# A decoder layer on one core: the SBUF layout of its matmul operands is changed

## The chip, the core and the metric

The kernel runs on one core of a Trainium2 chip. The metric is the time of one execution on the device in microseconds; lower is better. Of the core's engines, TensorE (PE) multiplies, VectorE (DVE) and ScalarE (ACT) work elementwise, GpSimd (POOL) does a few elementwise steps, and SyncE (SP) issues nearly all transfers from HBM into SBUF. PE reads its two operands from SBUF, the stationary one (a weight load, shown as PEld) and the moving one, and adds into PSUM.

## The reference, cut to what matters

One layer for 256 tokens of width 2048, all in float32 (S = 256, D = 2048, F = 5632):

```
h      = rms(x, norm1_g)
u, v, q, k, vr, g = split(h @ w_in)                # w_in: 2048 x 6144
y      = concat(spatial_gate(u, v), retention(q, k, vr, g))
x      = x + y @ w_out                             # 2048 x 2048
h2     = rms(x, norm2_g)
a      = silu(h2 @ w_gate) * (h2 @ w_up)           # two of 2048 x 5632
x      = x + a @ w_down                            # 5632 x 2048
return rms(x, final_norm_g)
```

The spatial gate and the retention work on chunks of 128 tokens and 8 heads each with 128 x 128 products; all else is the four large products.

## The kernel before

**One product as three.** A float32 product is made of three matmuls in the type float32r. Both factors are split: `hi` is the value cast to float32r, `lo` the rest. PE then adds `hi*hi`, `hi*lo` and `lo*hi` into one PSUM bank, always through the helper `mm` (line 42). The activations are the stationary factor (128 x 128, 512 bytes in each partition), the weights the moving one (128 x 512, 2048 bytes in each partition). `split` (line 44) makes `hi` on ScalarE (line 50) and `lo` on VectorE (line 51), into tiles of 1024 columns from a pool with four buffers each; the raw weights come in 1 MB tiles `raw` with three buffers (line 56).

**The stages.** `gemm_tok` (line 98) makes 12 blocks of 512 columns of w_in, with the activations in the tiles hT0 to hT3 (both parts of each), and then 4 blocks of w_out, with the activations in mT0 to mT3. Between them the small float32 products and transposes of the mixer are set in, on tiles `work` of 512 columns. `quad` (line 499) makes the FFN: 11 rounds over w_gate and w_up together, hT now holding h2, and 2 over w_down, with the split activations in hT0 to hT2.

**Seven for eight.** In each of the 11 rounds three of the eight pairs of row blocks (SEVEN_GU) go through `pair_seven` (line 471): sums and differences of the blocks are made first and seven products are taken for eight, as in Strassen's scheme. Four of the seven (3, 5, 7 and 6) have sums of activations as their stationary factor; these lie, split, in three tiles h2s1, h2s3 and h2s5 made once. Products 3, 5 and 7 follow each other, nine matmuls in a row. The tiles mT0 to mT3 serve as scratch there.

**What sets the order.** The engines work through their lists in the order in which the code is written; waits between them follow from the tiles. Where a tile lies in SBUF is set by the pools: a pool's tiles follow each other from its start, in the order of their first use, and the pools follow each other in the order in which they are opened. In the kernel before, the pool `base` is the first (line 36): the large tiles x, hT and mT (lines 87 to 89), then small ones (head, ident, ones, sums of squares, the scratch of the root), then `wp` (line 37) with raw, hi and lo, then the pool of the stage, `mix` (line 136) or `ff` (line 458).

Of the kernel before, what the change touches and what calls it, by code (L numbers as in the profile page):

```python
# [8 lines left out]
F32 = mybir.dt.float32  # L9
F32R = mybir.dt.float32r  # L10
# [5 lines left out]
P = 128  # L16
S = 256
NT = S // P
D = 2048
# [5 lines left out]
NC = 512  # L25
HC = NC // P
NF = DFF // NC
EPS = 1e-6
SEVEN_GU = (1, 3, 5)
WARM = 10  # L30

# [1 line left out]
@with_exitstack  # L33
def block_kernel(ctx: ExitStack, tc: tile.TileContext, a: dict, out: bass.AP):
    nc = tc.nc
    base = ctx.enter_context(tc.tile_pool(name="base", bufs=1))
    wp = ctx.enter_context(tc.tile_pool(name="wp", bufs=3))
    acc = ctx.enter_context(tc.tile_pool(name="acc", bufs=4, space=PSUM))
    sm = ctx.enter_context(tc.tile_pool(name="sm", bufs=4, space=PSUM))

# [19 lines left out]
    def rsqrt(v, n, pool):  # L60

        t = pool.tile([P, n], I32, name="rs_t", bufs=2, padded_shape=[P, 8])
        y = pool.tile([P, n], I32, name="rs_y", bufs=2, padded_shape=[P, 8])
        w = pool.tile([P, n], F32, name="rs_w", bufs=2, padded_shape=[P, 8])
        nc.vector.tensor_single_scalar(t, v.bitcast(I32), 1, op=ALU.logical_shift_right)
        nc.vector.tensor_scalar(out=y, in0=t, scalar1=-1.0, scalar2=float(0x5F3759DF), op0=ALU.mult, op1=ALU.add)
        yf = y.bitcast(F32)
        for i in range(3):
            r = pool.tile([P, n], F32, name="rs_r", bufs=6, padded_shape=[P, 8])
            nc.vector.tensor_tensor(out=w, in0=yf, in1=yf, op=ALU.mult)  # L70
            nc.vector.scalar_tensor_tensor(out=w, in0=w, scalar=-0.5, in1=v, op0=ALU.mult, op1=ALU.mult)  # L71
            nc.vector.scalar_tensor_tensor(out=r, in0=w, scalar=1.5, in1=yf, op0=ALU.add, op1=ALU.mult)  # L72
            yf = r
        return yf

    def row_rstd(parts, pool):
# [3 lines left out]
        nc.vector.tensor_reduce(out=v, in_=parts[:, 0:n - 1], op=ALU.add, axis=mybir.AxisListType.X)  # L80
        nc.vector.tensor_scalar(out=v, in0=v, scalar1=1.0 / D, scalar2=EPS, op0=ALU.mult, op1=ALU.add)
        w = pool.tile([P, 1], F32, name="rs_u", bufs=2)
# [1 line left out]
            out=w, in0=parts[:, n - 1:n], scalar1=1.0 / D, scalar2=v, op0=ALU.mult, op1=ALU.add)  # L84
        return rsqrt(w, 1, pool)

    x_sb = [base.tile([P, D], F32, name=f"x{n}") for n in range(NT)]
    hT = [base.tile([P, 4, 2 * S], F32R, name=f"hT{i}") for i in range(4)]
    mT = [base.tile([P, 4, 2 * S], F32R, name=f"mT{i}") for i in range(4)]
    head = base.tile([P, 2 * KD + 2 * S], F32, name="head")  # L90
    cols = head[:, 0:2 * KD]
    ident = base.tile([P, P], F32, name="ident")
# [144 lines left out]
    def norm_heads(src, dst, gi, half):  # L237
# [6 lines left out]
        for h in range(HC):  # L244
            nc.vector.bn_aggr(out=mv[:, h, :], in_=st[:, h, :])
        nc.vector.tensor_scalar(out=v, in0=mv[:, :, 1], scalar1=EPS, scalar2=None, op0=ALU.add)  # L246
        r = rsqrt(v, HC, mix)
# [180 lines left out]
    def turn_x(c):  # L428
        for half in range(2):
# [14 lines left out]
            p = 2 * c + half  # L444
            if p in SEVEN_GU:
                hf = ff.tile([P, 2, S], F32, name="hf", bufs=1)
# [5 lines left out]
    for c in range(4):  # L452
# [3 lines left out]
        if c == 0:  # L456
            p1.close()
            ff = ctx.enter_context(tc.tile_pool(name="ff", bufs=1))
            h2s = {p: ff.tile([P, 2, 4, P], F32R, name=f"h2s{p}") for p in SEVEN_GU}

# [4 lines left out]
    def pair_classic(src):  # L465

        return load_piece(src)

    odd = itertools.count()

    def pair_seven(src):

        raw = wp.tile([P, 2048], F32, name="raw", bufs=3)
        nc.sync.dma_start(raw, src)
        b12, b22, b21 = raw[:, 0:NC], raw[:, 2 * NC:3 * NC], raw[:, 3 * NC:]
        t = base.tile([P, 4 * NC], F32, name=f"mT{next(odd) % 2}")
        t13, t24 = t[:, 0:2 * NC], t[:, 2 * NC:]
        (plain,) = split(raw[:, NC:3 * NC], 2 * NC, 2 * NC)
        nc.vector.tensor_tensor(  # L479
            out=t13.rearrange("p (b c) -> p b c", b=2), in0=b12.unsqueeze(1).broadcast_to([P, 2, NC]),  # L480
            in1=raw[:, NC:3 * NC].rearrange("p (b c) -> p b c", b=2), op=ALU.subtract)
        nc.vector.tensor_tensor(out=t24[:, 0:NC], in0=b22, in1=t13[:, 0:NC], op=ALU.subtract)
        nc.vector.tensor_tensor(out=t24[:, NC:], in0=b21, in1=t24[:, 0:NC], op=ALU.subtract)
        (one,) = split(t13, 2 * NC, 2 * NC)
        (last,) = split(b21, NC, NC)
        (two,) = split(t24, 2 * NC, 2 * NC)
        cut = lambda part, h: tuple(x[:, h * NC:(h + 1) * NC] for x in part)
        return {1: cut(plain, 0), 3: cut(plain, 1), 5: cut(one, 0), 7: cut(one, 1),
                6: cut(two, 0), 4: cut(two, 1), 2: cut(last, 0)}
# [7 lines left out]
    odd_quad = itertools.count()  # L497

    def quad(src, order, seven, left, forms, todo=(), apart=0):


        todo = dict(todo)
        bank = {k: acc.tile([P, NC], F32, name="acc") for k in ("11", "12", "21", "22")}
        begun, mixed = set(), {}
        last7 = max([i for i, p in enumerate(order) if p in seven], default=-1)
        classic_left = [p for p in order if p not in seven]
        if seven:
            for k in (1, 5, 7, 6):
                bank[k] = sm.tile([P, NC], F32, name="sm")
        where = {1: 1, 2: "11", 3: "12", 4: "21", 5: 5, 6: 6, 7: 7}  # L510

        def go(b, l, r, stop):
            three(bank[b], l, r, b not in begun, stop)
            begun.add(b)

        kept = []
        for i, p in enumerate(order):
            for f in todo.get(i, ()):
                f()
            if p in seven:  # L520
                right = pair_seven(src(p))
                for k in (1, 3, 5, 7, 2, 6, 4) if i else (1, 5, 7, 6, 3, 2, 4):
                    whole = i == len(order) - 1 if isinstance(where[k], str) else i == last7
                    go(where[k], forms(p, k), right[k], whole)
                if i == last7:
                    t = base.tile([P, 4, NC], F32, name=f"mT{2 + next(odd_quad) % 2}")
                    t1, v, w, z = (t[:, i, :] for i in range(4))
                    nc.scalar.copy(t1, bank[1])
                    nc.vector.tensor_tensor(out=v, in0=bank[6], in1=t1, op=ALU.add)
                    nc.vector.tensor_tensor(out=w, in0=bank[5], in1=v, op=ALU.add)  # L530
                    nc.vector.tensor_tensor(out=z, in0=bank[7], in1=w, op=ALU.add)
                    nc.vector.tensor_tensor(out=v, in0=bank[7], in1=v, op=ALU.add)
                    mixed = {"11": t1, "12": w, "21": v, "22": z}
                continue
            (h0, l0), (h1, l1) = pair_classic(src(p))
            cut = lambda h, l, c: (h[:, c * NC:(c + 1) * NC], l[:, c * NC:(c + 1) * NC])
            right = {"12": cut(h0, l0, 0), "11": cut(h0, l0, 1), "22": cut(h1, l1, 0), "21": cut(h1, l1, 1)}
            todo_rows = [(p, right, i == len(order) - 1)]
            if i >= len(order) - apart:
                kept += todo_rows  # L540
                if i < len(order) - 1:
                    continue
                todo_rows, kept = kept, []
            for r in "12":
                for p_, right_, end in todo_rows:
                    for m in "12":
                        for c in "12":
                            go(r + c, left(p_, r + m), right_[m + c], end and m == "2")
        return bank, mixed
# [53 lines left out]
    for j in range(NF):  # L603
# [3 lines left out]
        else:  # L607
            todo[6] = [waiting]
        bank, mixed = quad(lambda p: a["w_gu"][j, p], range(KD // 2), SEVEN_GU, h2_left, h2_forms, todo)
        rows = finish_up(j, bank, mixed)  # L610
        waiting = lambda j=j, rows=rows: turn_a(j, rows)

    gf = base.tile([P, D], F32, name="hT3")
    nc.gpsimd.dma_start(gf, a["gf"].partition_broadcast(P))  # L614

    def a_split():

        made = {}

        def at(k, r):  # L620
            j = k // 4
            if j not in made:
                h = base.tile([P, 2, 4, S], F32R, name=f"hT{next(odd) % 3}")
                hi, lo = h[:, 0], h[:, 1]
                nc.scalar.copy(hi, af[j])  # L625
                nc.vector.tensor_tensor(out=lo, in0=af[j], in1=hi.bitcast(F32), op=ALU.subtract)  # L626
                made[j] = hi, lo
            return tuple(x[:, k % 4, r * P:(r + 1) * P] for x in made[j])

        return left_of(at)  # L630
# [116 lines left out]
```

## Time and profile before

| | |
|---|---|
| median of 3 runs | 1134.43 us (1134.06 to 1135.79) |
| the profiled execution | 1135.27 us, with a span of 1133.0 us |
| mean granted clock of TensorE | 0.995 of full speed |
| PE busy | 1116.5 us, 4937 instructions |
| VectorE busy | 814.0 us |
| ScalarE busy | 570.4 us |
| moved | 217.64 MB, 192 GB/s over the span |

The span runs from the first to the last instruction. Busy time is what an engine's own instructions cover; the chain that ended last is followed back from the last instruction, at each step to what released it, so its shares say on what the end rests. A PE instruction's duration covers the way through the array and overlaps the next one, so the pace of matmuls is read from how many start in a stretch, not from the mean of one.

### The profile page before, as it was taken

The page shows a single profiled execution, that of the slowest core. Times are in us where ns is not written, and L with a number is a line of the kernel's source. Part 1 is how long each engine was busy: PE and PEld are TensorE (multiplying, and loading weights), DVE is VectorE, ACT ScalarE, POOL GpSimd, SP SyncE. Part 2 cuts the span into 40 slices and gives each one's busy share as a digit, 9 for nine tenths or more (in the row PEclk, how much of TensorE's full clock was granted, in tenths as well). Part 3 has the DMA queues.
Part 4 walks back from the last instruction along what each step waited for, and adds up shares of the span by engine and source line. Part 5 has one row for each costly group of instructions (what it writes and reads, how often), then busy time and mean ns, then how long its engine had stood idle before and what let it go on. Part 6 is the DMA issues. An engine that isn't in the chain of part 4 may idle for free.

```text
span 1133.0 us, 12891 instructions
## 1 busy us (share of the span) xinstructions
PE 1116.5 (99%) x4937; PEld 901.4 (80%) x4937; DVE 814.0 (72%) x1097; ACT 570.4 (50%) x664; POOL 53.9 (5%) x36
## 2 busy tenths in 40 slices
PE   9989999999999999999999999999999999999996
PEld 7868888888888888888888888888888888888884
DVE  6896458476556689889888888888798555565555
ACT  6633434444345555556555555655656454454443
POOL 0051014011000000000000000000000000020000
PEclk9999999999999999999999999999999999999998
DMA  9845544445555445555645545555556555555551
GB/s 357 318 168 207 184 170 165 169 149 188 183 186 186 173 167 194 209 185 187 222 169 192 206 176 189 212 192 187 189 188 227 214 186 186 186 188 187 187 181 74
DMA packets 32749, 217.64 MB, mean 192 GB/s; under 512 B 3760, under 2 KB 4144, under 8 KB 7088
## 3 DMA queue, kind: packets, MB, share of 16 engines
q1 hardware_dynamic: 32544, 215.78, 53.5%
q0 software_dynamic: 144, 1.05, 0.2%
q8 instruction: 38, 0.62, 0.2%
q14 instruction: 23, 0.19, 0.0%
HBM read 214.72 MB, written 2.10 MB: 191 GB/s over the span
## 4 chain that ended last, share of the span: by engine, by line
PE 95%; DVE 3%; DMA 1%; ACT 1%; SPq 0%; issue 0%; DVEq 0%; ACTq 0%
PE acc L42 84%; PE sm L42 9%; PE sm L593 1%; DMA raw<-in_w_in 1%; DVE lo L51 1%; PE sm L434 0%; PE sm L329 0%; DVE rs_r L72 0%; DVE rs_w L71 0%; DVE work L249 0%; ACT junk L213 0%; PE sm L375 0%; ACT hi L50 0%; DVE var L246 0%; DVE x L648 0%
## 5 line engine op out<-in xcount | busy, mean ns | idle before, releaser
L42 PE MATMUL acc<-hi,hT 128*128 128x512 f32 x2484 | 799.6, 396 | 1.5 <-ACT hi L50 1.5
L51 DVE TENSOR_TENSOR lo<-raw,hi 128x1024 fp32r<-128x1024 f32 (+1 forms) x396 | 466.3, 1190 | 271.0 <-ACT hi L50 268.5
L50 ACT CAST hi<-raw 128x1024 fp32r<-128x1024 f32 (+1 forms) x396 | 395.8, 1009 | 466.1 <-PE acc L42 442.0
L42 PEld LDWEIGHTS acc<-hi,hT 128*128 128x128 f32 x2484 | 467.0, 188 | 113.5 <-ACT hi L50 2.2
L42 PE MATMUL acc<-lo,hT 128*128 128x512 f32 x1242 | 493.5, 397 | 3.4 <-DVE lo L51 3.4
L42 PEld LDWEIGHTS acc<-lo,hT 128*128 128x128 f32 x1242 | 233.6, 188 | 60.7 <-DVE lo L51 5.3
L51 DVE TENSOR_TENSOR lo<-mT,hi 128x1024 fp32r<-128x1024 f32 x66 | 80.7, 1223 | 18.2 <-ACT hi L50 18.0
L50 ACT CAST hi<-mT 128x1024 fp32r<-128x1024 f32 x66 | 69.4, 1051 | 33.2 <-PE acc L42 31.7
L42 PE MATMUL acc<-hi,mT 128*128 128x512 f32 x256 | 81.6, 396 | 0.1
L42 PE MATMUL sm<-hi,h2s 128*128 128x512 f32 x198 | 72.8, 394 | 0.0
L42 PEld LDWEIGHTS acc<-hi,mT 128*128 128x128 f32 x256 | 48.1, 188 | 12.0 <-ACT mT L378 0.5
L42 PE MATMUL acc<-lo,mT 128*128 128x512 f32 x128 | 50.5, 396 | 0.0
L42 PEld LDWEIGHTS sm<-hi,h2s 128*128 128x128 f32 x198 | 37.1, 188 | 9.0
L479 DVE TENSOR_TENSOR mT<-raw 128x1024 f32<-128x1024 f32 x33 | 40.3, 1222 | 1.0 <-DMA raw<-in_w_gu 0.5
L42 PE MATMUL sm<-lo,h2s 128*128 128x512 f32 x99 | 39.2, 396 | 0.0
L614 POOL DMA_DIRECT2D hT<-in_gf x1 | 0.7, 720 | 614.6 <-DVE mT L577 614.6
L42 PEld LDWEIGHTS acc<-lo,mT 128*128 128x128 f32 x128 | 24.0, 188 | 5.6
L626 DVE TENSOR_TENSOR hT<-af,hT 128x1024 fp32r<-128x1024 f32 x22 | 27.9, 1269 | 0.7 <-ACT hT L625 0.7
L582 ACT ACTIVATE sg<-mT,rstd 128x512 f32<-128x512 f32 x22 | 15.9, 723 | 24.0 <-DVE mT L577 24.0
L42 PE MATMUL acc<-hi,h2s 128*128 128x512 f32 x66 | 25.9, 392 | 0.0
L42 PE MATMUL sm<-hi,hT 128*128 128x512 f32 x66 | 25.9, 392 | 0.0
L625 ACT CAST hT<-af 128x1024 fp32r<-128x1024 f32 x22 | 22.9, 1042 | 0.0
(99 smaller groups left out, 545.1 us busy)
## 6 DMA issues: line engine op xcount, KB each, us to landing
raw<-in_w_gu SPq DMA_DIRECT2D x88, 1024.0 KB, 4.7
raw<-in_w_in SPq DMA_DIRECT2D x47, 1024.0 KB, 4.8
raw<-in_w_down SPq DMA_DIRECT2D x44, 1024.0 KB, 4.7
raw<-in_w_out SPq DMA_DIRECT2D x16, 1024.0 KB, 4.8
x<-in_x SPq DMA_DIRECT2D x2, 1024.0 KB, 9.2
gains<-in_gains SPq DMA_DIRECT2D x2, 1024.0 KB, 6.9
out<-x SPq DMA_DIRECT2D x8, 256.0 KB, 2.6
work<-in_xT SPq DMA_DIRECT2D x7, 256.0 KB, 7.7
```

The source lines that it names most:

```text
L42: nc.tensor.matmul(o, lhsT=l, rhs=r, start=start, stop=stop)
L50: nc.scalar.copy(hi, src[:, c:c + step])
L51: nc.vector.tensor_tensor(out=lo, in0=src[:, c:c + step], in1=hi.bitcast(F32), op=ALU.subtract)
L479: nc.vector.tensor_tensor(out=t13.rearrange("p (b c) -> p b c", b=2), in0=b12.unsqueeze(1).broadcast_to([P, 2, NC]), in1=raw[:, NC:3 * NC] ...
L582: nc.scalar.activation(sg, g, AF.Silu, scale=rstd2[r])
L593: nc.tensor.transpose(ps[:, q * S + n * P:q * S + (n + 1) * P], rows[n][:, f * P:(f + 1) * P], ident)
L614: nc.gpsimd.dma_start(gf, a["gf"].partition_broadcast(P))
L625: nc.scalar.copy(hi, af[j])
L626: nc.vector.tensor_tensor(out=lo, in0=af[j], in1=hi.bitcast(F32), op=ALU.subtract)
```

## The change

The constants `PAD_BIG` and `PAD_BASE` are new. A new pool `big` is opened first and takes x, hT and mT, behind a pad of 480 float32 columns; then comes `wp`, unchanged; then `base` with the small tiles, behind a pad of 40 columns; then the pool of the stage. Places that use the tiles of hT and mT again name the new pool. Tiles, sizes, number of buffers, engines and instructions are the same: on each of the five engines the list of instructions stands in the same order with the same waits; only the running numbers of the tiles are five higher.

```
+PAD_BIG = 480
+PAD_BASE = 40
...
+    big = ctx.enter_context(tc.tile_pool(name="big", bufs=1))
+    wp = ctx.enter_context(tc.tile_pool(name="wp", bufs=3))
     base = ctx.enter_context(tc.tile_pool(name="base", bufs=1))
-    wp = ctx.enter_context(tc.tile_pool(name="wp", bufs=3))
...
-    x_sb = [base.tile([P, D], F32, name=f"x{n}") for n in range(NT)]
-    hT = [base.tile([P, 4, 2 * S], F32R, name=f"hT{i}") for i in range(4)]
-    mT = [base.tile([P, 4, 2 * S], F32R, name=f"mT{i}") for i in range(4)]
+    big.tile([P, PAD_BIG], F32, name="pad_big")
+    base.tile([P, PAD_BASE], F32, name="pad_base")
+    x_sb = [big.tile([P, D], F32, name=f"x{n}") for n in range(NT)]
+    hT = [big.tile([P, 4, 2 * S], F32R, name=f"hT{i}") for i in range(4)]
+    mT = [big.tile([P, 4, 2 * S], F32R, name=f"mT{i}") for i in range(4)]
...
-        t = base.tile([P, 4 * NC], F32, name=f"mT{next(odd) % 2}")
+        t = big.tile([P, 4 * NC], F32, name=f"mT{next(odd) % 2}")
...
-    gf = base.tile([P, D], F32, name="hT3")
+    gf = big.tile([P, D], F32, name="hT3")
```

Where the tiles start in each partition, in bytes, in the two built programs:

| tile | used as | before | modulo 2048 | modulo 512 | after | modulo 2048 | modulo 512 |
|---|---|---|---|---|---|---|---|
| hT0 | stationary, float32r | 32896 | 128 | 128 | 34816 | 0 | 0 |
| mT0 | stationary, float32r | 65664 | 128 | 128 | 67584 | 0 | 0 |
| raw, first | weights as loaded | 102368 | 2016 | 480 | 100352 | 0 | 0 |
| hi, first | moving, float32r | 126944 | 2016 | 480 | 124928 | 0 | 0 |
| lo, first | moving, float32r | 143328 | 2016 | 480 | 141312 | 0 | 0 |
| h2s1 | stationary, float32r | 160736 | 992 | 480 | 162816 | 1024 | 0 |
| af0 | FFN activations, float32 | 177120 | 992 | 480 | 179200 | 1024 | 0 |
| ident | moving, float32 | 100608 | 256 | 256 | 161056 | 1312 | 288 |
| work, first | both, float32 | 160768 | 1024 | 0 | 162848 | 1056 | 32 |

The further tiles of a kind follow in steps of 8192 (hT, mT, raw), 4096 (hi, lo, h2s, af) and 2048 bytes (work).

## Rows read from the trace of the kernel before

**Rows 1.** The chain that ended last: shares of the span by engine, by line.
```profile
PE 95%; DVE 3%; DMA 1%; ACT 1%; SPq 0%; issue 0%; DVEq 0%; ACTq 0%
PE acc L42 84%; PE sm L42 9%; PE sm L593 1%; DMA raw<-in_w_in 1%; DVE lo L51 1%; PE sm L434 0%; PE sm L329 0%; DVE rs_r L72 0%; DVE rs_w L71 0%; DVE work L249 0%; ACT junk L213 0%; PE sm L375 0%; ACT hi L50 0%; DVE var L246 0%; DVE x L648 0%
```

**Rows 2.** Pieces of that chain, long ones: start us, us, what.
```profile
4.50 8.18 DMA raw<-in_w_in
...
119.81 22.40 PE acc L42 x96
...
361.88 22.41 PE acc L42 x96
...
909.78 206.53 PE acc L42 x885
```

**Rows 3.** Busy time by stretch: its length, each engine, clock, DMA share, GB/s.
```profile
25.00:50.00 25.00, 25.00 (x109) 20.10 (x108) 18.72 (x71) 16.12 (x27) 0.00 (x0) 1.00 0.85 334
...
700.00:800.00 100.00, 100.00 (x440) 80.51 (x439) 87.09 (x97) 57.17 (x63) 0.00 (x0) 1.00 0.53 188
1000.00:1100.00 100.00, 100.00 (x430) 80.47 (x429) 56.52 (x47) 47.19 (x49) 3.43 (x3) 1.00 0.52 186
```

**Rows 4.** Pieces of the chain around products 3, 5 and 7 (h2s).
```profile
403.36 1.37 PE sm L42 x6
...
446.20 0.69 PE acc L42 x3
446.89 1.39 PE sm L42 x6
448.29 0.70 PE acc L42 x3
...
449.69 6.30 PE acc L42 x27
```

**Rows 5.** Pieces of the chain: small float32 products, transposes.
```profile
93.86 0.87 PE sm L329 x8
...
142.21 2.68 PE sm L42 x24
```

**Rows 6.** A matmul and the next weight load in order of time: start, us.
```profile
200.04 0.62 PE L42 MATMUL acc<-hi,hT 128*128 128x512 f32 x2
200.04 0.19 PEld L42 LDWEIGHTS acc<-hi,hT 128*128 128x128 f32 x1
```

**Rows 7.** PE's instructions by form: count, busy us, mean ns of one.
```profile
L42 PEld LDWEIGHTS acc<-hi,hT 128*128 128x128 f32 x2484 | 467.0, 188 | 113.5 <-ACT hi L50 2.2
...
L42 PE MATMUL sm<-hi,h2s 128*128 128x512 f32 x198 | 72.8, 394 | 0.0
...
L42 PE MATMUL sm<-lo,h2s 128*128 128x512 f32 x99 | 39.2, 396 | 0.0
...
L42 PE MATMUL acc<-hi,h2s 128*128 128x512 f32 x66 | 25.9, 392 | 0.0
...
L42 PE MATMUL acc<-lo,h2s 128*128 128x512 f32 x33 | 13.1, 397 | 0.0
...
L42 PEld LDWEIGHTS sm<-work 128*128 128x128 f32 x96 | 11.3, 192 | 0.4
```

**Rows 8.** VectorE's instructions by form, 1024 columns: count, busy us, mean ns.
```profile
L51 DVE TENSOR_TENSOR lo<-raw,hi 128x1024 fp32r<-128x1024 f32 x355 | 438.2, 1247 | 228.9 <-ACT hi L50 227.5
...
L51 DVE TENSOR_TENSOR lo<-mT,hi 128x1024 fp32r<-128x1024 f32 x66 | 80.7, 1223 | 18.2 <-ACT hi L50 18.0
...
L626 DVE TENSOR_TENSOR hT<-af,hT 128x1024 fp32r<-128x1024 f32 x22 | 27.9, 1269 | 0.7 <-ACT hT L625 0.7
```

**Rows 9.** Who waited for whom: us in total, times, longest.
```profile
ACT hi L50 <- PE acc L42: 473.7, 319, 5.5
...
PE acc L42 <- DVE lo L51: 3.4, 3, 1.9
```

**Rows 10.** Transfers by line: count, KB each, median us from issue to landing.
```profile
raw<-in_w_down SPq DMA_DIRECT2D x44, 1024.0 KB, 4.7
...
hT<-in_gf POOLq DMA_DIRECT2D x1, 1024.0 KB, 5.2
```

More of the change, by code (lines that the diff above doesn't have):

```diff
@@ L525, in quad @@
                 if i == last7:
-                    t = base.tile([P, 4, NC], F32, name=f"mT{2 + next(odd_quad) % 2}")
+                    t = big.tile([P, 4, NC], F32, name=f"mT{2 + next(odd_quad) % 2}")
                     t1, v, w, z = (t[:, i, :] for i in range(4))
@@ L622, in at @@
             if j not in made:
-                h = base.tile([P, 2, 4, S], F32R, name=f"hT{next(odd) % 3}")
+                h = big.tile([P, 2, 4, S], F32R, name=f"hT{next(odd) % 3}")
                 hi, lo = h[:, 0], h[:, 1]
```

## The prediction

> **What bounds the kernel now.** I read the chain of work that ended last first, then its pieces in order of time, then busy time by stretch, then single forms of instructions. "Phase" below is a tile's start address modulo 512 bytes, from the address table in the section on the change.
>
> TensorE is 95% of the chain, and the helper line 42 alone, on the two kinds of PSUM tile, is 84% + 9% [rows 1]. 93% of the 1133.0 us span is 1054 us; with the granted clock at 1.00 in the stretches of [rows 3], the engine is at its 2.4 GHz level there and does not stand. So the time is the pace of the matmuls, and little else. The reader is to see in [rows 2] that the pace is one number: 96 matmuls in 22.40 us is 233.3 ns each, with tile hT stationary; 22.41 us with mT stationary; 885 in 206.53 us is 233.4 ns near the end. 512 columns at 2.4 GHz would be 213.3 ns, so each matmul carries 20 ns that are not columns.
>
> What else runs beside does not touch this pace: the DMA share goes from 0.85 to 0.52 and VectorE's busy time from 87 to 57 us per 100, while PE is busy in all of each stretch [rows 3]. The other engines follow PE: ScalarE's high parts wait 473.7 us for PE to free a buffer, PE's matmuls wait 3.4 us for VectorE's low parts [rows 9]. A change of layout can therefore move the time in one way that counts: by the 20 ns.
>
> **The change part by part.**
>
> *Instructions.* None is added, removed or moved; every engine's list is the same but for tile numbers, and every wait with it. The removal of a wait, or a new one, costs 0 because there is none.
>
> *Stationary and moving operands of the float32r matmuls.* Before, the moving operand (hi, lo) always starts at phase 480; the stationary one starts at phase 128 in hT and mT and at phase 480 in the three sum tiles h2s. After, all start at phase 0. So before has two kinds of matmul: phases that differ (hT, mT) and phases that coincide (h2s), and after has only the second kind, though at another place. [Rows 4] show what that is worth in one Strassen-like piece: the matmuls of h2s come as 3 in 0.69 us and 6 in 1.39 us, 2.08 us for 9 or 231.1 ns; by the starts (446.20 to 448.29) 2.09 us or 232.2 ns. The 27 that follow, with hT stationary, take 6.30 us, 233.3 ns. In another piece the 6 take 1.37 us, 228.3 ns. I take 231.5 ns for coinciding phases, 1.8 ns under 233.3 (0.8%).
>
> How many would gain: of 1054 us on line 42 I take off 128 small float32 matmuls (24 take 2.68 us, 111.7 ns each [rows 5], so 14.3 us) and the 198 + 99 + 66 + 33 = 396 matmuls with h2s [rows 7], which have that pace already (396 x 231.5 ns = 91.7 us). That leaves 948 us, and 0.8% of it is 7.3 us (948 x 1.8 / 233.3). That is the term of the forecast: -7.3 us. Its ends: 0 if the h2s tiles are quicker for another reason (their phase 480 itself, or that they lie some 100 KB higher than hT), and then these 396 could lose their 1.8 ns, +0.7 us; and on the other side the whole of the 20 ns, 948 x 20 / 233.3 = -81 us, because no row shows a moving operand of 512 columns at any other phase than 480. Above, the nearest row is the 4 ns that a weight load takes longer where everything starts at phase 0 (192 against 188 ns [rows 7]): 948 + 92 us, times 4 / 233.3, is +17.8 us. I take the value that a row of the same kind of matmul shows.
>
> *The small float32 matmuls and transposes.* The work tiles go the other way, from phase 0 to phase 32, ident from 256 to 288. At phase 0 moving, 111.7 ns; transposes with ident moving at phase 256, 8 in 0.87 us or 108.8 ns [rows 5]. The 2.9 ns between is the bound on both sides: 128 x 2.9 ns = 0.4 us more or less; I take 0.
>
> *VectorE and ScalarE.* Their operands change phase too. Forms of 1024 columns whose operands' phases agree (raw, hi, lo, all 480) take 1247 ns, mixed ones (mT 128, hi 480) 1223 ns, and hT 128 with af 480 take 1269 ns [rows 8]: a spread of 46 ns with no order in it by phase. At worst 355 low parts by 22 ns and 66 by 46 ns, 10.8 us over the whole span, 1% on VectorE's 87 us per 100 in its fullest stretch [rows 3]. PE's matmuls cover it: VectorE would have to become 14% slower to be the bound. 0 on the path.
>
> *DMA.* Weight rows land at 32 modulo 64 before and at a multiple of 2048 after. Only the first pieces are on the chain, 8.18 us [rows 2]; later ones land while PE works. No row has the same transfer at two addresses. The nearest are transfers of 1024 KB that land at phase 480 (raw, 4.7 us) and at phase 128 (the gains in hT3, 5.2 us, issued from another queue) [rows 10]: a tenth, so 0.8 us of the 8.18 either way at most, and I take 0.
>
> A page bears on this one. The Trainium skill, "DMA: Bandwidth & Descriptors", section "How a descriptor splits into AXI transactions", says that a descriptor not starting on a multiple of 256 bytes pays an extra transaction for the start. By it a 2048-byte row at 224 modulo 256 takes 9 transactions for 8; my estimate from that page is up to a tenth of 8.18 us, 0.8 us, so the sum would be 0.8 us lower. No row of this trace shows it.
>
> *Sum.* The profiled execution took 1135.27 us, its span 1133.0, and the median of the three runs is 1134.43. The term is made on the span and taken from the median: 1134.4 - 7.3 = 1127.1, and I forecast 1127 us.
>
> **The rivals.**
>
> *No change: 1134.* For it: the pace with hT is the same whether the stationary slice starts at 128, 640, 1152 or 1664 modulo 2048, and the same for hT and mT, 32 KB apart [rows 2]; so most address changes that the trace contains do nothing. Against it: h2s is not at 233.3. If its gain is from its own phase, the sum is +0.7 and at most 0.4 from the small ones, 1134 to 1135.5.
>
> The Trainium skill speaks for this rival: "SBUF — State Buffer", section "Specifications (TRN2)", gives lines of 16 bytes, where each cross to a new line pays a penalty. All starts were multiples of 32 before and are after, so by that rule no operand crosses more lines than it did, and the time would be 1134. The trace agrees for hT and mT, whose paces are equal [rows 2], and disagrees by 0.8% for h2s [rows 4].
>
> *The moving operand's start is most of the 20 ns: 1066.* A float32 matmul of 128 columns that starts at phase 0 has 111.7 ns, 5.0 more than 106.7 (twice 128 columns at 2.4 GHz). If float32r then also carried 5 ns and not 20, the gain is 948 + 92 us times 15 / 233.3, 67 us, so 1067. A third of it gives 1112. Against it: transposes whose moving operand starts at phase 256, off every multiple of 512, are no slower, so a start that is off a multiple costs nothing there.
>
> "TensorE: Matmul & The Clock Gate", section "Back-to-back issue gap", in the Trainium skill gives about 216 ns for 512 columns when issued back to back. By it, 17 of the 20 ns are an extra of this kernel, and the time would be 1040 x 17.3 / 233.3 = 77 us lower, an estimate from that page. The trace does not reach it anywhere: its quickest pieces are at 228 ns.
>
> *Slower: 1152.* The load of the next weights starts with the matmul (200.04 us both, [rows 6]) and takes 188 ns of the 233. Now both read streams begin at the same offset of 2048 bytes, always. If they meet in the same part of the memory and take turns, the load is longer, as in the phase-0 rows (192 ns against 188 [rows 7]), and a load that ends 4 ns later may hold the next matmul by as much: +17.8 us, 1152. It decides from the point where the load has no slack; it has 45 ns now, which speaks against, and so do the h2s matmuls, which coincide modulo 512 and are the quickest. Halfway, 1143.
>
> That the change does not do what it says is excluded: the addresses in the table are those of the built program.
>
> **How the numbers follow.** Chances: the forecast (all matmuls at the pace of h2s, 1122 to 1131) 0.35; no change 0.34; the large gain (under 1122) 0.14; slower 0.17. Forecast and no change are nearly equal; the gains together are likelier than either, so the time is that of the likelier gain. About 0.2% (2.3 us) is what a measurement of this kernel can tell from no change. Faster by more: 0.35 + 0.14 less what of the forecast's case ends within 2.3 us (0.03), 0.46. Within: 0.34 + 0.03, 0.37. Slower: 0.17. The range for 8 in 10 leaves out the deep part of the large gain (below 1108, about 0.1) and the far half of the slower case (above 1141, about 0.09). The forecast's own range is 1122 to 1131.
>
> **What would show it.** Right: in the pieces of the chain 96 matmuls with hT take 22.2 us and the last long piece loses 1.6 us of 206.5, while the h2s pieces stay at 1.39 us and the forms of VectorE within the spread of [rows 8]. No change: 22.40 us again, and h2s pieces at 1.40. Large gain: 22.40 us falls to 21 or below, and then VectorE's waits for PE shrink in the middle stretches, where it has least room. Slower: 22.4 grows and weight loads show more than 188 ns. I am wrong in mechanism, whatever the time, if the pace of hT stays and the time moves, for then a stretch without line 42 did it.

## The result and the profile after

The changed kernel takes 1107.77 us (median of 4 runs, 1106.7 to 1108.37) against 1134.98 us for the kernel before in the same runs (median of 4): 0.9759 of it, with a 95% interval of 0.9743 to 0.9776, or 27.2 us less. The forecast was 1127 us. The profiled execution took 1108.35 us, with a span of 1106.1 us. One profiled execution in the experiments below, that of the third, took 3223 us, and no figure here is made from it. Lines of the program stand 3 to 5 further down: line 42 is now 45, lines 50 and 51 are 53 and 54.

The chain by engine still is TensorE [rows 1]:

```profile
PE 95%; DVE 2%; DMA 1%; ACT 0%; SPq 0%; issue 0%; DVEq 0%; ACTq 0%
```

Its long pieces in order of time (start us, us, what) answer to [rows 2], and the one of 24 small matmuls to [rows 5]:

```profile
4.49 8.43 DMA raw<-in_w_in
...
73.40 12.62 PE acc L45 x47
...
118.59 21.80 PE acc L45 x96
140.39 2.68 PE sm L45 x24
...
354.51 21.80 PE acc L45 x96
...
888.87 200.66 PE acc L45 x885
```

96 matmuls take 21.80 us where they took 22.40, and 885 take 200.66 where they took 206.53: 226.7 ns each, 6.6 less than 233.3. The small float32 matmuls keep their 2.68 us for 24 (two instructions for each of 12 in the code), although their tiles moved from a multiple of 512 to 32 past it. Around products 3, 5 and 7 (to [rows 4]):

```profile
436.77 0.68 PE acc L45 x3
437.45 1.36 PE sm L45 x6
438.81 0.68 PE acc L45 x3
...
440.17 6.12 PE acc L45 x27
```

The h2s matmuls, which I expected to stay at 1.39 us for 6, went to 1.36: they have the same 226.7 ns as all others now. Product 6 has sums as its stationary factor too, but only three matmuls, and they stand alone between matmuls of hT. [Rows 4] leave it out; here it is, before and after:

```profile
448.99 0.70 PE sm L42 x3
...
439.49 0.68 PE sm L45 x3
```

Before, these three were as slow as hT, 0.70 us or 233 ns each, although their starts agreed. Weight loads by form [rows 7] and VectorE's forms [rows 8] (count, busy us, mean ns of one):

```profile
L45 PEld LDWEIGHTS acc<-hi,hT 128*128 128x128 f32 x2484 | 467.3, 188 | 98.4 <-ACT hi L53 2.3
...
L54 DVE TENSOR_TENSOR lo<-raw,hi 128x1024 fp32r<-128x1024 f32 x355 | 435.2, 1239 | 213.9 <-ACT hi L53 207.5
...
L54 DVE TENSOR_TENSOR lo<-mT,hi 128x1024 fp32r<-128x1024 f32 x66 | 80.6, 1220 | 16.1 <-ACT hi L53 16.1
...
L631 DVE TENSOR_TENSOR hT<-af,hT 128x1024 fp32r<-128x1024 f32 x22 | 27.9, 1267 | 0.7 <-ACT hT L630 0.7
```

A weight load still takes 188 ns, and VectorE's forms are within 8 ns of what they were. What moved the time is the pace of the float32r matmuls. Priced with the prediction's own shares, 948 us x 6.6 / 233.3 and 92 us of h2s x 4.8 / 231.5 are 26.8 + 1.9 = 28.7 us; the span lost 26.9. Most of the rest stays in the first 120 us: the piece that starts there starts 1.2 us earlier (118.59 for 119.81), where the pace alone would give up to 3.0 us on the 106 us since the first matmul of the chain. Before 73 us PE waits for VectorE's chain of statistics, so the next long piece begins at 73.40 us instead of 73.69; before it read:

```profile
73.69 12.78 PE acc L42 x47
```

### The profile page after: what moved, and what is told of

The parts are those of the page before. It is cut to its first block, busy times and chain, and to the rows that moved or that the text cites. A ratio compares the mean times of both kernels' runs of the same rounds, so it can differ in the third digit from the quotient of the medians.

```text
span 1106.1 us, 12891 instructions
## 1 busy us (share of the span) xinstructions
PE 1088.6 (98%) x4937; PEld 901.6 (82%) x4937; DVE 810.6 (73%) x1097; ACT 570.2 (52%) x664; POOL 55.0 (5%) x36
## 4 chain that ended last, share of the span: by engine, by line
PE 95%; DVE 2%; DMA 1%; ACT 0%; SPq 0%; issue 0%; DVEq 0%; ACTq 0%
PE acc L45 84%; PE sm L45 9%; PE sm L598 1%; DMA raw<-in_w_in 1%; DVE lo L54 1%; PE sm L439 0%; PE sm L334 0%; ACT junk L218 0%; DVE rs_r L75 0%; DVE rs_w L74 0%; PE sm L380 0%; DVE work L254 0%; DVE x L653 0%; SPq L168 0%; DVE rs_w L73 0%
## 5 line engine op out<-in xcount | busy, mean ns | idle before, releaser
L45 PE MATMUL acc<-hi,hT 128*128 128x512 f32 x2484 | 786.6, 391 | 1.9 <-ACT hi L53 1.9
L45 PE MATMUL acc<-lo,hT 128*128 128x512 f32 x1242 | 484.7, 390 | 4.1 <-DVE lo L54 4.1
L258 POOL TENSOR_TENSOR work<-work,gains 128x512 f32<-128x512 f32 x8 | 17.5, 2192 | 124.1 <-DVE work L254 62.1
```

Of the source, the lines that this page charges most:

```text
L45: nc.tensor.matmul(o, lhsT=l, rhs=r, start=start, stop=stop)
L258: nc.gpsimd.tensor_tensor(out=dst, in0=dst, in1=gains[gi][:, 0, cs], op=ALU.mult)
```

## The experiments

For the theories, d is the start of the stationary operand less that of the moving one, modulo 256 bytes. Before, d is 160 for hT and mT (128 - 224) and 0 for h2s (224 - 224). After, it is 0 everywhere. The first four runs were made to tell whether the moving operand alone, the stationary one alone or the pair decides.

**Moving operands 32 bytes off.**

```
-PAD_BASE = 40
+PAD_BASE = 32
+    wp.tile([P, 8], F32, name="pad_wp", bufs=1)        # opens the pool of weight buffers
```

> The changed layout with 32 bytes put ahead of the weight buffers: hi, lo and raw start at 32 modulo 2048, everything else stays where the change put it (stationary tiles at multiples of 512). Theory M (the start of the moving operand modulo 64 decides; one that is off by 32 costs 16 columns): 96 matmuls take 22.4 us again (233.3 ns each), time 1132 to 1137 us. Rival C (what counts is that the two operands start at the same offset modulo 512): now they differ everywhere, also slow, 1132 to 1137 us, and the sum products are slow as well, at 1.40 us for 6. Rival S (the stationary tiles alone made the gain): 21.8 us for 96, 1106 to 1110 us.

Measured: 1135.4 us, 0.9996 of before (0.9987 to 1.0005). The long last piece of the chain and one of h2s:

```profile
446.81 1.40 PE sm L45 x6
...
910.11 206.51 PE acc L45 x885
```

All of the gain is gone, at 233.3 ns, h2s included. Theories M and C both expected this; theory S, the stationary tiles alone, is out.

**Stationary tiles at eight starts, moving ones at 0.** hT and mT are made one by one with a pad ahead of each:

```
...
+    for name, cols in (("hT0", 0), ("hT1", 8), ("hT2", 24), ("hT3", 56), ("mT0", 8), ("mT1", 8), ("mT2", 8), ("mT3", 48)):
+        if cols:
+            big.tile([P, cols], F32, name=f"pad_{name}")
+        (hT if name[0] == "h" else mT).append(big.tile([P, 4, 2 * S], F32R, name=name))
...
```

> The changed layout, moving operands kept on multiples of 2048, but the stationary tiles each at its own start modulo 512: hT0 to hT3 at 128, 160, 256 and 480, mT0 to mT3 at 0, 32, 64 and 256. Theory M: every one of the eight at 226.7 ns, 24 matmuls of each in 5.44 us, time 1106 to 1110 us. Rival C: only mT0 at 226.7 ns, the others near 233; time about 1130. Rival S: those at 0, 64, 128 and 256 at 226.7, those at 32, 160 and 480 (off a multiple of 64) at 233 ns; about 1120 us.

Measured: 1126.95 us, 0.9931 (0.991 to 0.9952), a time that none of the three theories gave. From the chain, 24 matmuls each of hT3 (start 480), hT0 (128) and mT3 (256), in this order:

```profile
123.62 5.60 PE acc L44 x24
...
129.22 5.59 PE acc L44 x24
...
305.78 5.47 PE acc L44 x24
```

5.47 us is 228 ns, the others 233. So the moving operand's start is not enough either: theory M is out. Rival S is out too, since 128 is slow. The moving operands stay where they are in this kernel and the pace goes with the stationary tile, so it is not the writing or the landing of the weights that sets it. 256 is nearly as good as 0 (228 ns for mT3, 226.7 for mT0, which follows it), so rival C is left, with 256 in place of 512.

The h2s tiles lie at 0 here, so they match; what differs is the hT tile before and behind them. Six matmuls of products 5 and 7 between those of hT0 (128), of hT1 (160) and of hT2 (256):

```profile
443.02 1.37 PE sm L44 x6
...
453.48 1.39 PE sm L44 x6
...
463.81 1.36 PE sm L44 x6
```

With the same matching starts, nine h2s matmuls run at 232 ns between neighbours that are off by 160, at about 227.5 between neighbours off by 128, and at 226.7 between neighbours that match; this holds for all rounds but the first.

**Moving operands 64 bytes off.** As the first, with 16 columns and 24.

> The changed layout with 64 bytes put ahead of the weight buffers: hi, lo and raw start at 64 modulo 2048. Theory M in its form with 64 bytes: 226.7 ns, 1106 to 1110 us, although every moving operand now runs over a multiple of 2048, 512 and 256. Theory M with a larger unit (128 bytes or more): 233.3 ns, 1132 to 1137 us. Rival C: the operands' offsets differ by 64, so near 233 ns, 1132 to 1137 us.

Measured: 1115.36 us (the median of three executions, 1115.24 to 1118.8), 0.9834 (0.9813 to 0.9855), between the two values that the theories allowed. The 1117 us that an expectation below names for this kernel is the median with the 3223 us counted in. There is no trace of one of the three. 20.1 us less than before, over the 4605 float32r matmuls, is 4.4 ns each, so 229 ns a matmul if all have it; the mix below shows which pairs have that.

**The old order with 32 bytes.**

```
+    wp.tile([P, 8], F32, name="pad_wp", bufs=1)        # in the kernel before
```

> The kernel before with one edit: a pad of 8 float32 columns (32 bytes) ahead of the weight buffers, which brings hi, lo and raw from 2016 to 0 modulo 2048; hT and mT stay at 128 modulo 512, the order of the pools is the old one, small tiles shift by 32 bytes. Theory M: the whole gain, 1106 to 1110 us. Rival C: hT and mT still differ from the moving ones, so no gain there, 1132 to 1137 us. Rival O (the order of the pools, large tiles first, matters): 1132 to 1137 us.

Measured: 1131.09 us, 0.9966 (0.9952 to 0.9979). The end piece:

```profile
906.48 205.67 PE acc L42 x885
```

232.4 ns, 1.0 less than before: with d = 128 the moving operands on multiples of 2048 bring little, and the whole gain of theory M is not there. The h2s tiles came to 0 by the same pad, so they match, and 6 of theirs take 1.37 us, 228 ns each, between neighbours that do not match:

```profile
445.54 1.37 PE sm L42 x6
```

Both are part of the 4 us gained, which put the time a little under the 1132 us of the rivals. That left theory K, equal starts modulo 256 wherever they lie, against theory A, each operand on a multiple of its own.

**The moving operands at 128, 32, 64 and 256, with eight starts of stationary tiles.** One kernel each; the diff is that of the second experiment with other pads.

> The changed layout with the eight stationary tiles at eight starts modulo 512: hT0 to hT3 at 128, 256, 0 and 64, mT0 to mT3 at 160, 384, 480 and 32, and hi, lo and raw at 128 modulo 2048; the sum tiles h2s at 0. Read are the paces of each tile's matmuls. Theory K (the two operands must start at the same offset modulo 256, wherever that is): hT0 (128) and mT1 (384) at 226.7 ns, all others near 233, h2s too. Theory A (each operand for itself must start on a multiple of its own unit, 256 bytes for the stationary one, 64 or 256 for the moving one): hT0 and mT1 near 233 ns; with a moving unit of 64 or 128 hT1, hT2 and h2s (256, 0, 0) at 226.7, with 256 nothing at 226.7.

> As the kernel with the moving operands at 128, but hi, lo and raw at 32 modulo 2048. Theory K: only mT3 (32) at 226.7 ns. Theory A: nothing at 226.7 ns, all near 233, mT3 included.

> As the kernel with the moving operands at 128, but hi, lo and raw at 64 modulo 2048. Theory K: only hT3 (64) at 226.7 ns. Theory A with a moving unit of 64: hT1, hT2 and h2s at 226.7 ns and hT3 near 233; with a larger unit hT1, hT2 and h2s between 227 and 233, as the first kernel with 64 (time 1117 us) lets expect, and hT3 slower than these.

> As the kernel with the moving operands at 128, but hi, lo and raw at 256 modulo 2048. Theory K and theory A with a unit of 256 or less: hT1, hT2 and h2s (256, 0, 0) at 226.7 ns, all others near 233. If the moving operand needs a multiple of 512 or 2048, nothing is at 226.7 ns.

Measured: 1126.2, 1135.47, 1125.72 and 1120.7 us (0.9924, 1.0003, 0.9924 and 0.988 of before, each with an interval of at most 0.003 to either side). Pieces of the chain with 24 matmuls of one tile. Moving at 128, stationary at 64, 128 and 256:

```profile
175.10 5.50 PE acc L44 x24
...
180.59 5.46 PE acc L44 x24
...
186.06 5.58 PE acc L44 x24
```

Moving at 32, stationary at 128 and 32:

```profile
132.28 5.61 PE acc L44 x24
...
309.71 5.44 PE acc L44 x24
```

Moving at 256, stationary (hT1) at 256:

```profile
135.67 5.45 PE acc L44 x24
```

The pair 32 and 32, off every multiple of 64, is as quick as the pair 256 and 256, and 128 with 256, both on multiples of 128, is slow. So theory A is out and theory K is met, with one exception: it expected 233 ns for all pairs that differ, and 64 with 128 (d = 192) took 5.50 us, 229 ns. By d, the pace of every 24 matmuls in a row of one tile with no gap over 260 ns between two starts, after 120 us, in these four kernels and in the second (time from the first start to the last in the trace, over 23; ns):

| d | 0 | 32 | 64 | 96 | 128 | 160 | 192 | 224 |
|---|---|---|---|---|---|---|---|---|
| median | 226.9 | 233.2 | 233.4 | 234.0 | 232.7 | 233.4 | 229.3 | 233.3 |
| lowest | 226.7 | 233.1 | 232.9 | 232.2 | 232.1 | 233.0 | 228.7 | 232.8 |
| highest | 228.7 | 233.4 | 233.5 | 234.6 | 233.5 | 233.9 | 233.3 | 233.5 |
| rows of 24 | 146 | 27 | 59 | 41 | 127 | 41 | 80 | 84 |

At 192 there are two paces: 45 of the 80 rows are under 231 ns, 35 over it. The starts do not tell them apart: with the moving operands at 64, hT1 in the w_down rounds runs at 229.1 ns from 878.67 us on, at 233.3 when its turn comes again at 912.74, at 229.1 at 946.33, and so on. What switches it is open. 192 is also the d of the third experiment, with its 1115 us.

**All operands at 224.** The kernel before, with two pads:

```
+    base.tile([P, 24], F32, name="pad_a")              # ahead of x, hT, mT
...
+    base.tile([P, 40], F32, name="pad_b")              # behind them
```

> The order of the pools as before, with a pad of 96 bytes ahead of the large tiles and one of 160 behind them, so that hT, mT, h2s, hi, lo and raw all start at 224 modulo 256: the same offset, and off every multiple of 64. Theory K (equal offsets modulo 256 are all that counts): 226.7 ns in the whole program, h2s included, 1106 to 1110 us; the 231 ns of h2s before were then nine matmuls that had not settled. Theory A (both operands on multiples of 256): 1132 to 1137 us. Theory H (coinciding offsets away from a multiple give only the 231.5 ns that h2s had before): 1126 to 1129 us.

**The change without its pads.** The lines with `PAD_BIG` and `PAD_BASE` are left out.

> The change without its two pads: only the order of the pools is new. hT, mT, hi, lo and raw then all start at 128 modulo 256 by themselves, h2s at 224. Theory K: 226.7 ns for hT and mT, about 233 for the 396 matmuls of h2s (6 in 1.40 us), time 1109 to 1113 us. Theory A: 1132 to 1137 us.

**Small operands too**, and the changed kernel beside it:

```
-PAD_BASE = 40
+PAD_BASE = 32
...
+            ff.tile([P, 8], F32, name="pad_ff")        # ahead of h2s
```

> The changed layout with 8 columns less in the second pad and 8 more ahead of h2s, so that the operands of the small float32 matmuls and transposes (work, const8, ident) start at 0 modulo 256 as well, not at 32. Theory K for float32r alone: no difference from the changed kernel, 1106 to 1109 us. Rival: the small matmuls and the few disturbed float32r matmuls next to them gain too, at most 130 x 3 ns and 60 x 10 ns, 1 us less.

> The changed kernel as it is, for comparison on the same chip: 1106 to 1109 us.

Measured: 1107.12 us with all at 224 (0.9762, 0.9746 to 0.9779), 1109.7 without pads (0.9785, 0.977 to 0.9799), 1107.85 with the small ones and 1106.88 for the changed kernel again. All at 224:

```profile
446.28 1.36 PE sm L42 x6
...
887.55 200.63 PE acc L42 x885
```

Without pads, where hT, mT and the weights start at 128 and h2s at 224:

```profile
447.70 1.40 PE sm L43 x6
...
891.59 200.63 PE acc L43 x885
```

Every figure of theory K came out here: full gain off any alignment, full gain from the order alone, and h2s alone at 233 where it alone differs. The new order of the pools made the starts equal by itself, since hT, mT, raw, hi and lo all have sizes that are multiples of 2048 and now follow each other; the pads bring h2s into line, 2 to 3 us. The small operands bring nothing. No version tried is quicker than the changed kernel by more than the runs differ.

**Which pair: the matmul with its own weights, or with those being loaded?** The lo tiles of the weights were moved to 128; in the w_down rounds lo of the activations too:

```
...
+                shifted.append(wp.tile([P, 32], F32, name="pad_lo", bufs=1))
...
-                h = big.tile([P, 2, 4, S], F32R, name=f"hT{next(odd) % 3}")
-                hi, lo = h[:, 0], h[:, 1]
+                h = big.tile([P, 8 * S + 64], F32R, name=f"hT{next(odd) % 3}")
+                hi, lo = (h[:, o:o + 4 * S].rearrange("p (k s) -> p k s", k=4) for o in (0, 4 * S + 32))
```

> The changed layout with lo of the weights at 128 modulo 256 (hi at 0), and in the two rounds over w_down, near the end, lo of the activations at 128 too (hi at 0). Each product's three matmuls are then, there, moving 0 with stationary 0, moving 128 with stationary 0, moving 0 with stationary 128; while each runs, the next weights are loaded: from 0, from 128, from 0. Theory L (a matmul's moving operand must start like the stationary operand that is being loaded while it runs): all three agree, 226.7 ns in the w_down rounds, 200.7 us for 885. Theory P (it must start like its own stationary operand, loaded before): two of three differ, 231 ns or more, 204 us or more. In the earlier stages lo of the activations stays at 0, one of three differs by either theory, so 228 to 233 ns and a time of 1110 to 1130 us.

Measured: 1128.79 us, 0.9945 (0.9928 to 0.9961). Two pieces of the rounds over w_gate and w_up, then the end piece, in the w_down rounds:

```profile
447.25 6.30 PE acc L45 x27
...
490.71 6.23 PE acc L45 x27
...
905.32 204.54 PE acc L45 x885
```

The end piece has 231.1 ns, so the 226.7 of theory L does not come and P's figure is met. But P is not shown. Where one of three matmuls had d = 128 by either theory, whole rounds ran at 233 ns and whole rounds at 231, with the same starts: no better than where two of three had it by P. The price does not add up matmul by matmul; one odd operand in three loses two thirds of the gain or all of it. And this is the only kernel in which hi and lo of the weights, two moving operands that follow each other, start differently; whether that costs something by itself, which would leave room for theory L, was not tried.

## Why the prediction was right and wrong

*What bounds the kernel* was right: the pace of the float32r matmuls is nearly the whole difference, and no form read of another engine moved by more than 8 ns.

*The mechanism* was right: what counts is whether the two operands start at the same offset, h2s had it and hT had not. The runs make it sharper (modulo 256, at any offset) and exclude the two readings that would have taken it away, that h2s were quick for their own phase 480 or for lying higher: with h2s still at 224 modulo 256 but the weights at 128, they are slow, 1.40 us for 6.

*The term was mis-sized, and this is the step that failed*: "I take 231.5 ns for coinciding phases, 1.8 ns under 233.3". It is 226.7 ns, 6.6 ns under, so the term was -26.8 us and not -7.3. I took for the settled pace what nine matmuls with equal starts had between others with unequal ones. The experiment with all at 224 gives the same h2s, at the same offset of 224, neighbours that match, and they go from 1.39 to 1.36 us: the neighbours had spoilt them. It was not that nine are too few: between neighbours off by 128 nine were nearly as quick as a uniform stream (1.37 us for 6), between neighbours off by 160, as they were before, they had 1.39 in the second experiment too. The 1.37 us of one piece [rows 4] was a sign of it, and so were product 6's three at 0.70 us, which the rows leave out: the same kind of matmul had three paces, and I averaged two where I had to ask which was the disturbed one.

*The 92 us of h2s left out as already quick* gained more by the same reason, about 1.9 us by the prediction's prices; 99 of these 396 matmuls, product 6's, were not even quick.

*Small matmuls, VectorE, ScalarE* at 0: right, 2.68 us as before and forms within 8 ns.

*DMA* at 0: the first transfer on the chain took 8.43 us for 8.18, and 8.59 in the repeated run of the changed kernel. Over the seven traced kernels in which it lands on a multiple of 256 it took 7.90 to 8.75 us, over the seven others 8.11 to 8.83: no gain, within a spread of 0.9 us. The Trainium skill's page "DMA: Bandwidth & Descriptors" ("How a descriptor splits into AXI transactions") had let me estimate up to 0.8 us less; the runs do not show it. The page speaks of what a transaction reads, and what moved here is where it writes.

*The rivals.* No change fell. Its first argument carried nothing: 128, 640, 1152 and 1664 are all 128 modulo 512, one phase and not four. The rule of "SBUF — State Buffer" in the Trainium skill, on crossings of 16-byte lines, does not account for the result: every start in every kernel is a multiple of 32, and the pace ran from 226.7 to 234.6 ns. Slower fell: loads kept 188 ns, and starting at the same offset is the best case, not the worst. The time lies in the range of the large gain (under 1122), if far from its own 1066 (1067 by its sum), but not by its cause: moving operands on multiples of 2048 with hT left at 128 brought 1.0 ns (205.67 us for 885), and in that d went from 160 to 128. The 216 ns of "TensorE: Matmul & The Clock Gate" in the Trainium skill, which the section "Back-to-back issue gap" itself calls the gap of an isolated matmul, was reached by no kernel here; 226.7 ns is the least for a settled run.

*The range* ended at 1108 and the time is 1107.77: its low end hung on that other cause, with a chance of 0.14, while the forecast's own mechanism had been given no room to be larger than its one sample.

## What to carry to other kernels

Where float32r matmuls set the pace, give the tiles of both operands the same start modulo 256 bytes, for instance by taking them from pools that follow each other and hold only tiles of 2048-byte multiples; alignment to large powers of two is not needed. Where hi and lo take turns, all of them have to agree, not most. And when a trace shows a cheaper sample of a thing only in short runs among dearer ones, a uniform stream may gain more than the sample: here 6.6 ns and not 1.8.

## What was not expected of the hardware

The pace of 512-column float32r matmuls depends on the difference of two SBUF addresses modulo 256 and not on either address alone: 226.7 ns at d = 0 in a stream that keeps to it, 229 or 233 at 192, 232 to 235 at the other six multiples of 32. At 2.4 GHz that is 544, 550 and 560 columns' time for 512 columns. It is a property of the stream rather than of one matmul: matching matmuls had 227, 232 or 233 ns by their neighbours, and at d = 192 and with one odd operand in three the same starts gave two paces. Which shared part of the machine makes it is open; no run here separates the reading of the weights from that of the moving operand any further than the last experiment did. The 128-column float32 matmuls were not tested for it: their work tiles moved together, from 0 to 32, so d among them stayed 0, and 2.68 us for 24 says nothing on unequal starts.
